# The first stage of a hybrid trunk kernel: adaLN modulation as column sums for three feature tiles and row sums for five, with two head pairs projected tile by tile

## The chip, the cores and the metric

The kernel runs on one core of one Trainium2 chip. The metric is the device time of one execution in microseconds, the median of several runs. The core has five engines that run side by side, each through its own instructions in order: TensorE (PE, matmuls), ScalarE (ACT), VectorE (DVE), GpSimd (POOL) and SyncE (SP), which here issues all transfers between memory and the on-chip buffers. Engines wait for each other through semaphores.

## The reference

One layer of a transformer trunk (DEPTH = 1, so the mixer is stick-breaking attention): 2048 tokens, 1024 features, 16 heads of 64, all float32.

```python
mod_all = jnp.einsum('bd,lde->lbe', jax.nn.silu(c), ada_w) + ada_b[:, None]
sh_m, sc_m, gt_m, sh_f, sc_f, gt_f = jnp.split(mod_all[i][:, None, :], 6, axis=-1)
h = modulate(rms_norm(x, norm_g[i, 0]), sh_m, sc_m)     # h * (1 + scale) + shift
qkv = h @ w_qkv
...
z = q @ k^T * scale ; a = exp(z - reverse_cumsum(softplus(z)))  (masked) ; o = a @ v
...
x = x + gt_m * rms_norm(o @ w_o, norm_g[i, 1])
h = modulate(rms_norm(x, norm_g[i, 2]), sh_f, sc_f)
x = x + gt_f * rms_norm((silu(h @ w_g) * (h @ w_u)) @ w_out, norm_g[i, 3])
```

The change concerns the first three lines and the first two head pairs of the fourth.

## The kernel before

Sequence blocks are 512 tokens wide (`BT`, four blocks `b`), features come in eight tiles of 128 (`KC`, index `k` or `m`), heads in eight pairs `p`. A float32 product is done as three matmuls of rounded high halves and residual low halves (`mm3`, L174): high by high, high by low, low by high. So each operand is split: ACT rounds the high half, DVE subtracts it to get the low half. PE, ACT, DVE and POOL run in the order in which the program text calls them (`manual_schedule`); SP's order is left to the framework. Tiles come from pools by tag with a fixed number of buffers (`BUFS`); taking a buffer whose last user is not done means a wait. SP has eight semaphores for its transfers in turn, so it issues a transfer once the one eight places earlier has landed.

A step `(p, b)` projects one pair's K (`t=1`), Q (`t=0`) and V (`t=2`) for one block, in that order: 3 × 8 × 3 = 72 matmuls, `project` (L453). The steps run (0,0), (1,0), (0,1), (0,2), (0,3) and so on. Step (1,0) is "parked": block 0's normalised input is at hand, so pair 1 is projected with it and its K, Q and V go to memory until pair 1's turn. After each product, `split` (L505) takes one of two buffers with the tag `qkn`, ACT and DVE write its halves, and SP copies them into K's or Q's own layout (four transfers each, L524 and L538) or to memory (parked).

The first stage is what comes ahead of the attention:

- Modulation: shift and scale are `silu(c) @ ada_w` for 2 × 1024 columns, 8 MB of weights. Before, they come in four quarters `q` of two feature tiles (`ada_chunk`, L701). For each quarter DVE sums `c[k]` times row chunk `k` over the chunks into a 128 × 512 sum (`ada_sum`, L719: L724 and L727), PE multiplies the last chunk directly (`ada_direct`, L734: L737) and sums the DVE sums over the partitions (`ada_rest`, L742: L744). Each such matmul has 128 × 128 weights and a single moving column. `ada_cols_done` (L749) adds the biases and makes the gains.
- Block 0: tokens are loaded (`x_load`), their mean squares taken on ACT (`x_square`), scaled on DVE (`x_scale`), transposed on PE (`x_turn`, L367), given gain and shift on ACT (`full_high`, L776), and split (`low`, L789). `first_products` (L768) adds tile `m` to pair 0's three accumulators. The loop over `q` interleaves the sums for the next quarter with the products of this one.
- Step (1,0) then runs as an ordinary step from the stored halves. Its weights come through `split_early` (L207). Around its matmuls lie block 0's stores, block 1's squares and normalisation, and block 2's squares (`SQUARE_AT`).
- Blocks 1 and 3 are normalised from a transposed copy of `x` (`cols_load`, tag `kt`): `x_share` (L355) turns the per-token factors into a row spread over all partitions with four transposes, `scale_cols` (L377) multiplies (even tiles on DVE, odd ones on POOL), and `modulate` (L389) adds the shift and splits. `first_norm` (L420) strings these together, one tile at a time.

Of the kernel before, what the change touches and what calls it, by code (L numbers as in the profile page):

```python
# [9 lines left out]
F32 = mybir.dt.float32  # L10
# [29 lines left out]
SLICES = [0, 3 * KC] + [3 * KC + VGAP] * (NPAIR * NB - 2)  # L40


AHEAD = 6 * KC + 6
# [4 lines left out]

AQ = 256
# [25 lines left out]
SQUARE_AT = [(0, 2), (0, 7), (2, 1), (2, 7)]  # L75

NORM_AT = {
    None: [], 1: [(0, 4), (0, 6), (2, 3), (2, 5)],
    2: [(2, 2), (2, 4), (2, 6)], 3: [(2, 2), (2, 4), (2, 6)],
}  # L80
# [27 lines left out]
def hybrid_trunk_kernel(  # L108
# [5 lines left out]
    ada_first: bass.AP,  # L114
# [28 lines left out]
    shift = const.tile([P, 2, KC], F32, name="shift")  # L143
    c_act = const.tile([P, KC], F32, name="c_act")
# [61 lines left out]

    def split_early(p, t, tags):  # L207

        raw = raws.pop((p, t))
        if len(tags) == 1:  # L210
            hl = att.tile([P, 2, KC, P], F32R, name=f"w{p}_{t}", tag=tags[0], bufs=BUFS[tags[0]])
            hi, lo = hl[:, 0], hl[:, 1]
        else:
            hi, lo = [
                att.tile([P, KC, P], F32R, name=f"w{p}_{t}_{j}", tag=tag, bufs=BUFS[tag])
                for j, tag in enumerate(tags)
            ]
        nc.scalar.copy(hi, raw)
        nc.vector.tensor_tensor(lo, raw, f32(hi), op=ALU.subtract)
        weights[p, t] = hi, lo  # L220

# [86 lines left out]

    def x_load(b):
        for i in range(4):  # L310
            r0 = b * BT + i * P
            if b == 2:
                if i % 2 == 0:
                    pair = att.tile([P, 2, D], F32, name=f"x{b}_{i}", tag="qt", bufs=BUFS["qt"])
                tok = pair[:, i % 2]
# [5 lines left out]
    def cols_load(b):  # L321
        for m in range(KC // 2):
# [54 lines left out]
    def scale_cols(b, k):  # L377
# [4 lines left out]
        if k % 2 == 0:  # L382
# [6 lines left out]
    def modulate(hl, b, k):  # L389

        gain, add = g_eff[:, 0, k : k + 1], shift[:, 0, k : k + 1]
# [7 lines left out]
        if k % 2 == 0:  # L399
# [53 lines left out]
    def project(at):  # L453

        p, b = STEPS[at]
        begun = (p, b) == (0, 0)
# [7 lines left out]
        def product(t):  # L464
            if begun:
                return first_acc[t]
            w = weights[p, t]
            if parked and t == 1:
                acc = zps.tile([P, BT], F32, name=f"pj{p}_{b}_{t}", tag="z")
            else:  # L470
                acc = accps.tile([P, BT], F32, name=f"pj{p}_{b}_{t}", tag="acc")
            ahead = b == NB - 1 and p + 1 < NPAIR
            for k in range(KC):
                if t == 1:
# [4 lines left out]
                    if k == 5 and waiting:  # L479
                        waiting.pop()()  # L480
                if parked and t == 1 and k % 2 == 0:
                    nc.sync.dma_start(*stores[k // 2])
                if parked and (t, k) == (1, 6):
                    split_early(1, 2, ["whl"])
                if nb in (1, 3) and t == 1 and k < 4:
                    x_square(nb, k)
                if nb and t == 1 and 2 <= k < 6:
                    x_spread(nb, k - 2)
                if nb == 2 and (t, k) == (0, 0):
                    x_load(3)  # L490
                if nb == 1 and (t, k) in SQUARE_AT:
                    x_square(2, SQUARE_AT.index((t, k)))
                if nb and (t, k) == (0, 1):
                    x_share(nb)
                if (t, k) in NORM_AT[nb]:
                    first_norm(nb, NORM_AT[nb].index((t, k)))
# [37 lines left out]
        else:  # L534
# [6 lines left out]
            queries[p, b] = qt  # L541

# [154 lines left out]
    chunks, piece_sums, cols_ps = {}, {}, {}  # L697

    ON_PE = {0: (0, KC - 1), 1: (KC - 1,), 2: (KC - 1,), 3: (KC - 1,)}

    def ada_chunk(q, kh):  # L701
        ks = range(KC // 2 * kh, KC // 2 * (kh + 1))
        if q == 2:
            for k in ks:
                w = att.tile([P, 2, AQ], F32, name=f"ac{q}_{k}", tag="a", bufs=BUFS["a"])
                nc.sync.dma_start(w, ada_first[q, kh][:, :, k % 4])
                chunks[q, k] = w
            return
        tag = "ht" if (q, kh) == (1, 1) else "qt"
        w = att.tile([P, 2, KC // 2, AQ], F32, name=f"ac{q}_{kh}", tag=tag, bufs=BUFS[tag])  # L710
        nc.sync.dma_start(w, ada_first[q, kh])
        for k in ks:
            chunks[q, k] = w[:, :, k % 4]

    def ada_begin(q):
        cols_ps[q] = zps.tile([P, BT], F32, name=f"acol{q}", tag="z")
        nc.vector.memset(cols_ps[q][:, :4], 0.0)

    def ada_sum(q, k):  # L719
        w, scale = chunks[q, k], c_act[:, k : k + 1]  # L720
        if q not in piece_sums:
            acc = att.tile([P, 2, AQ], F32, name=f"asum{q}", tag="w", bufs=BUFS["w"])
            piece_sums[q] = acc
            nc.vector.tensor_scalar(acc, w, scale, None, op0=ALU.mult)  # L724
        else:
            acc = piece_sums[q]
            nc.vector.scalar_tensor_tensor(acc, w, scale, acc, op0=ALU.mult, op1=ALU.add)  # L727

    def ada_sums(q):
        return [k for k in range(KC) if k not in ON_PE[q]]  # L730

    COLUMNS = [(2 * seg + j, seg, slice(j * P, (j + 1) * P)) for seg in range(2) for j in range(2)]

    def ada_direct(q, k):  # L734

        for n, seg, js in COLUMNS:
            nc.tensor.matmul(  # L737
                cols_ps[q][:, n : n + 1], chunks[q, k][:, seg, js], c_act[:, k : k + 1],
                start=False, stop=False, skip_group_check=True,
            )  # L740

    def ada_rest(q):  # L742
        for n, seg, js in COLUMNS:
            nc.tensor.matmul(  # L744
                cols_ps[q][:, n : n + 1], piece_sums[q][:, seg, js], ones[:, 0:1],
                start=False, stop=n == 3, skip_group_check=True,
            )

    def ada_cols_done(q):  # L749

        ps, ms = cols_ps.pop(q), slice(2 * q, 2 * q + 2)
        nc.vector.tensor_tensor(shift[:, 0, ms], ps[:, 0:2], b_cols[:, 0, ms], op=ALU.add)
        sc = att.tile([P, KC], F32, name=f"sc0_{q}", tag="sc", bufs=1)[:, :2]
        nc.vector.tensor_tensor(sc, ps[:, 2:4], b_cols[:, 1, ms], op=ALU.add)
        nc.vector.scalar_tensor_tensor(
            g_eff[:, 0, ms], sc, 1.0, gc[:, 0, ms], op0=ALU.add, op1=ALU.mult
        )

    def weights_high(t):
        hl = att.tile([P, 2, KC, P], F32R, name=f"w0_{t}", tag="whl", bufs=BUFS["whl"])  # L760
        nc.scalar.copy(hl[:, 0], raws[0, t])
        weights[0, t] = hl[:, 0], hl[:, 1]

    def weights_low(t):
        hi, lo = weights[0, t]
        nc.vector.tensor_tensor(lo, raws.pop((0, t)), f32(hi), op=ALU.subtract)
# [918 lines left out]
```

## Time and profile before

| | |
|---|---|
| median of 3 runs | 2847.76 us (2846.84 to 2848.67) |
| the profiled execution | 2848.15 us, of which its span is 2845.8 us |
| PE busy (matmul) | 2795.2 us, 98% of the span |
| DVE, ACT, POOL busy | 71%, 57%, 45% |
| HBM traffic | 165 GB/s over the span |
| first 20 us: PE, DVE, ACT busy | 8.33, 9.79, 10.55 us |
| DMA in the first 100 us | 366 GB/s |

How to read it: a timeline row gives the start in us, the time it took, the engine, the line, the operation, output <- inputs, the shape, how many were merged (`x8`), and in brackets how long the engine had been idle and what released it. Consecutive matmuls overlap in these rows, so their pace is the distance between starts. An f32 matmul shows as two rows. `PEld` is the loading of weights, `SPq` SP's issue of a transfer. In the views by stretch, after the length come PE's busy time with the number of rows in parentheses, the granted clock of PE as a share of the full one, the busy share of the DMA engines and GB/s.

### The profile page before, as it was taken

The page shows a single profiled execution, that of the slowest core. Times are in us where ns is not written, and L with a number is a line of the kernel's source. Part 1 is how long each engine was busy: PE and PEld are TensorE (multiplying, and loading weights), DVE is VectorE, ACT ScalarE, POOL GpSimd, SP SyncE. Part 2 cuts the span into 40 slices and gives each one's busy share as a digit, 9 for nine tenths or more (in the row PEclk, how much of TensorE's full clock was granted, in tenths as well). Part 3 has the DMA queues.
Part 4 walks back from the last instruction along what each step waited for, and adds up shares of the span by engine and source line. Part 5 has one row for each costly group of instructions (what it writes and reads, how often), then busy time and mean ns, then how long its engine had stood idle before and what let it go on. Part 6 is the DMA issues. An engine that isn't in the chain of part 4 may idle for free.

```text
span 2845.8 us, 41691 instructions
## 1 busy us (share of the span) xinstructions
PE 2795.2 (98%) x13792; PEld 2330.7 (82%) x13792; DVE 2028.9 (71%) x2821; ACT 1634.1 (57%) x3273; POOL 1289.3 (45%) x2036
## 2 busy tenths in 40 slices
PE   8899999999999999999999999999999999999998
PEld 6688888888888888887888788888788888888887
DVE  6788888888888888888866766555775665133477
ACT  5787777787787877878645533333433333322343
POOL 2575666676576655666410122222222222544455
PEclk9999999999999999999999999999999999999999
DMA  9874556656665635546289544334353334545565
GB/s 368 283 225 164 185 161 221 211 178 226 193 211 186 216 114 178 193 134 230 95 296 317 195 141 151 119 106 158 124 177 108 111 108 163 191 142 155 179 224 185
DMA packets 240519, 521.03 MB, mean 183 GB/s; under 512 B 22448, under 2 KB 110512, under 8 KB 222640
## 3 DMA queue, kind: packets, MB, share of 16 engines
q1 hardware_dynamic: 240304, 518.38, 56.2%
q8 instruction: 109, 1.79, 0.3%
q14 instruction: 106, 0.87, 0.1%
HBM read 351.04 MB, written 118.49 MB: 165 GB/s over the span
## 4 chain that ended last, share of the span: by engine, by line
PE 86%; DVE 5%; ACT 3%; issue 2%; POOL 2%; DMA 2%; SPq 0%; DVEq 0%; POOLq 0%; ACTq 0%
PE s L176 9%; PE s L178 9%; PE s L177 9%; PE z L604 8%; PE o L683 8%; PE t L655 8%; PE pj L176 5%; PE pj L177 5%; PE pj L178 5%; PE o L177 4%; PE o L176 4%; PE o L178 4%; PE y L178 2%; PE y L176 2%; PE y L177 2%
## 5 line engine op out<-in xcount | busy, mean ns | idle before, releaser
L645 POOL TENSOR_TENSOR a<-a,w 128x512 f32<-128x512 f32 (+3 forms) x640 | 621.1, 970 | 225.2 <-DVE w L638 128.9
L638 DVE TENSOR_TENSOR_SCAN w<-z,c,begin 128x512 f32<-128x512 f32 x384 | 489.3, 1278 | 84.6 <-ACT z L623 62.2
L176 PE MATMUL s<-r,l 128*128 128x512 f32 x1232 | 482.2, 391 | 4.8 <-DVE p L1447 3.9
L178 PE MATMUL s<-r,l 128*128 128x512 f32 x1232 | 479.9, 390 | 0.0
L177 PE MATMUL s<-r,l 128*128 128x512 f32 x1232 | 479.9, 390 | 0.0
L621 ACT ACTIVATE a<-z 128x512 f32<-128x512 f32 (+3 forms) x640 | 347.4, 543 | 170.4 <-PE z L604 137.7
L683 PE MATMUL o<-aT,v 128*128 128x512 f32 (+3 forms) x1280 | 384.3, 381 | 0.1
L671 DVE TENSOR_TENSOR aT<-t,aT 128x512 fp32r<-128x512 f32 (+3 forms) x640 | 358.6, 594 | 23.7 <-ACT aT L665 23.0
L604 PE MATMUL z<-kt,qt 128*128 128x512 f32 (+3 forms) x1280 | 363.0, 365 | 0.1
L665 ACT CAST aT<-t 128x512 fp32r<-128x512 f32 (+3 forms) x640 | 314.1, 534 | 73.4 <-PE t L655 63.2
L623 ACT ACTIVATE z<-z 128x512 f32<-128x512 f32 (+3 forms) x640 | 345.0, 539 | 0.0
L1455 POOL TENSOR_TENSOR one<-p,p 128x512 f32<-128x512 f32 x44 | 71.6, 1627 | 578.1 <-issue 321.7
L176 PE MATMUL pj<-ht,w 128*128 128x512 f32 x768 | 309.1, 402 | 5.0 <-issue 1.4
L655 PE MATMUL t<-begin,a 128*128 128x128 f32 x2176 | 295.2, 273 | 14.3 <-DVE aT L671 13.0
L655 PEld LDWEIGHTS t<-begin,a 128*128 128x128 f32 x2176 | 254.7, 140 | 65.1 <-DVE aT L671 15.5
L177 PE MATMUL pj<-ht,w 128*128 128x512 f32 x768 | 303.4, 395 | 1.8 <-DVE ht L408 0.5
L178 PE MATMUL pj<-ht,w 128*128 128x512 f32 x768 | 302.8, 394 | 0.0
L176 PEld LDWEIGHTS s<-r,l 128*128 128x128 f32 x1232 | 231.7, 188 | 54.8 <-ACT l L1308 2.9
L178 PEld LDWEIGHTS s<-r,l 128*128 128x128 f32 x1232 | 231.6, 188 | 48.4
L177 PEld LDWEIGHTS s<-r,l 128*128 128x128 f32 x1232 | 231.8, 188 | 48.2 <-issue 0.5
L633 DVE TENSOR_TENSOR_SCAN w<-z,begin 128x128 f32<-128x128 f32 (+3 forms) x256 | 208.6, 817 | 76.9 <-ACT z L623 66.0
L604 PEld LDWEIGHTS z<-kt,qt 128*128 128x128 f32 x1280 | 230.3, 188 | 37.8 <-DVE w L633 0.5
(178 smaller groups left out, 4866.6 us busy)
## 6 DMA issues: line engine op xcount, KB each, us to landing
ht<-h_s SPq DMA_DIRECT2D x108, 1024.0 KB, 8.4
wi<-in_win SPq DMA_DIRECT2D x86, 512.0 KB, 4.0
qt<-qn SPq DMA_DIRECT2D x124, 256.0 KB, 4.6
ol_qt<-act_s SPq DMA_DIRECT2D x56, 512.0 KB, 3.7
act_s<-S SPq DMA_DIRECT2D x66, 256.0 KB, 3.9
br<-in_wout SPq DMA_DIRECT2D x66, 256.0 KB, 3.5
h_s<-ht SPq DMA_DIRECT2D x16, 1024.0 KB, 8.3
o_s<-os SPq DMA_DIRECT2D x128, 128.0 KB, 2.8
```

Source lines behind the costliest of these rows:

```text
L176: nc.tensor.matmul(acc, lhs[0], rhs[0], start=first, stop=False, **kw)
L177: nc.tensor.matmul(acc, lhs[0], rhs[1], start=False, stop=False, **kw)
L178: nc.tensor.matmul(acc, lhs[1], rhs[0], start=False, stop=last, **kw)
L604: nc.tensor.matmul(z[:, :n], q[:, e, part, r * P : (r + 1) * P], k[:, e, :n], start=part == 0, stop=part == 1,)
L621: nc.scalar.activation(a[:, :n], z[:, :n], AF.Sigmoid, scale=QK_SCALE)
L623: nc.scalar.activation(z[:, :n], z[:, :n], AF.Sigmoid, scale=-QK_SCALE)
L638: nc.vector.tensor_tensor_scan(rest[:, rev], left[:, rev], begin[:, :BT][:, rev], initial=carries[r], op0=ALU.mult, op1=ALU.bypass,)
L645: nc.gpsimd.tensor_tensor(a[:, :n], a[:, :n], rest[:, 1 : n + 1], op=ALU.mult)
L655: nc.tensor.transpose(pt[:, rb * P : (rb + 1) * P], weighed[i, rb][:, j * P : (j + 1) * P], ident)
L665: nc.scalar.copy(hl[:, 0, t0:], pt[:, t0:])
L671: nc.vector.tensor_tensor(hl[:, 1, t0:], pt[:, t0:], f32(hl[:, 0, t0:]), op=ALU.subtract)
L683: nc.tensor.matmul(acc[:, t0:], lhs, hl[:, part, t0:], start=sc == qb and j == 0 and part == 0, stop=sc == 0 and j == 3 and part == 1,)
```

## The change

Modulation by feature tile `m`, not by quarter. Tiles 0 to 2 (`COLUMNS = 3`) are summed on PE alone: for shift and scale each eight matmuls with a single moving column, into one PSUM tile `acol`. Tiles 3 to 7 come with `ada_w` transposed, features on partitions, and DVE multiplies a 128 × 1024 tile by `silu(c)` spread over all partitions and accumulates along the row in one instruction (`row_sum`); the spread `c_rows` is made by two PE matmuls of ones and `c_line` (`c_spread`) and copied by ACT. `row_load` makes two loads of 512 KB for a tile, shift and scale. `row_done` makes `mod` and `g_eff` of one tile.

```diff
-    def ada_chunk(q, kh):
...
-    def ada_cols_done(q):
...
+    ROW_TAGS = {0: "whl", 1: "qt", 2: "qt", 3: "qt", 4: "ht", 5: "ht"}
+    def row_load(m):
...
+    def column(m, seg):
+        w = rows[m][seg].rearrange("p (k f) -> p k f", f=P)
+        out_col = acol[:, 2 * m + seg : 2 * m + seg + 1]
+        for k in range(KC):
+            nc.tensor.matmul(out_col, w[:, k], c_act[:, k : k + 1], start=k == 0, stop=k == KC - 1)
+    def row_sum(m, seg):
+        nc.vector.scalar_tensor_tensor(
+            w, w, 1.0, c_rows, op0=ALU.mult, op1=ALU.mult, accum_out=sums[m][:, seg : seg + 1])
+    def row_done(m):
+        total = acol[:, 2 * m : 2 * m + 2] if m < COLUMNS else sums.pop(m)
+        nc.vector.tensor_tensor(mod[:, :, m], total, b_cols[:, 0:2, m], op=ALU.add)
+        nc.vector.scalar_tensor_tensor(g_eff[:, 0, m : m + 1], mod[:, 1, m : m + 1], 1.0, ...)
```

Both pairs' products of block 0 are then made tile by tile, with six accumulators (pair 1's in the three buffers of `zps`): `products(p, m, *ts)` in place of `first_products(m)`, and steps (0,0) and (1,0) no longer yield (`begun = at < 2`, `SLICES = [0, 0, ...]`). The loop over `q` gives way to a list of calls. Its core:

```diff
+    column(0, 0); column(0, 1)
...
+    column(1, 0); column(1, 1)
+    turn_x(0); turn_x(1); row_done(1)
+    weights_high(0, 1); full(0); weights_low(0, 1); weights_high(0, 0); high(0); full(1)
+    turn_x(2); weights_low(0, 0)
+    column(2, 0)
+    low(0); weights_high(0, 2); turn_x(3); weights_low(0, 2)
+    products(0, 0, 1, 0)
+    high(1); weights_high(1, 1); low(1)
+    column(2, 1)
+    products(0, 0, 2); products(0, 1, 1)
+    weights_low(1, 1); row_done(2); weights_high(1, 0)
+    products(1, 0, 1); products(0, 1, 0)
...
+    products(0, 2)
+    row_sum(4, 0); row_sum(4, 1); row_done(4); low(3); full(4); high(4)
+    products(1, 2)
...
+    products(0, 6)
+    x_share(1)
+    products(1, 6)
+    products(0, 7)
+    first_norm(1, 0); first_norm(1, 1)
+    products(1, 7)
```

In `project`, pair 0's K and Q splits are each preceded by one more `first_norm` of block 1, the loads of block 2 and two stores of block 0 follow pair 0's Q, and `split` for pair 1 (parked) comes right behind. The two V turns run at `k` = 3 and 5 of step (0,1)'s K product. Block 2's squares move from step (1,0) to the Q product of step (0,1).

```diff
         def product(t):
             if begun:
-                return first_acc[t]
+                if at == 0 and t != 2:
+                    first_norm(1, 2 + (t == 0))
+                return first_acc[p, t]
...
-                    if k == 5 and waiting:
-                        waiting.pop()()
+                    if k in (3, 5) and waiting:
+                        waiting.pop(0)()
...
-                if nb in (1, 3) and t == 1 and k < 4:
+                square_at = {2: 0, 3: 1}.get(nb)
+                if t == square_at and k < 4:
                     x_square(nb, k)
...
+        if at == 0:
+            x_load(2)
+            store(2)
+            store(3)
```

For block 1, `scale_cols` and `modulate` treat all tiles as the even ones were (`if k % 2 == 0 or b == 1`): DVE scales, ACT adds the shift and rounds, DVE makes the low half. Buffers change hands: the raw weights of pair 1 take the tag `v`, those of pair 0's V the tag `kt`, `c_line` and `c_rows` the tag `qkn`. SP's order in the changed kernel is: tile 0's rows, `c`, block 0's tokens, biases, tile 1's rows, pair 0's weights, tile 2's rows, pair 1's weights, the rows of tiles 3 to 7, then block 1's transposed copy and tokens and block 0's stores. The attention and everything behind it are unchanged.

More of the change, by code (lines that the diff above doesn't have):

```diff
@@ L47 @@
 EAGER = 12
-AQ = 256
 BUFS = {
@@ L764, in weights_low @@
[L764 to L770 removed]
+                out_col, w[:, k], c_act[:, k : k + 1], start=k == 0, stop=k == KC - 1,
+            )
+    def row_sum(m, seg):
+        w = rows[m][seg]
+        if m not in sums:
+            sums[m] = att.tile([P, 2], F32, name=f"as{m}", tag="as", bufs=3)
+        nc.vector.scalar_tensor_tensor(
+            w, w, 1.0, c_rows, op0=ALU.mult, op1=ALU.mult, accum_out=sums[m][:, seg : seg + 1]
+        )
@@ L824, in hybrid_trunk_kernel @@
+    column(0, 1)
+    c_spread = [zps.tile([P, BT], F32, name=f"cs{half}", tag="z") for half in range(2)]
+    for half in range(2):
+        nc.tensor.matmul(
+            c_spread[half], ones, c_line[:, half * BT : (half + 1) * BT], start=True, stop=True
+        )
+    c_rows = att.tile([P, D], F32, name="c_rows", tag="qkn", bufs=BUFS["qkn"])
+    x_square(0, 0)
+    row_done(0)
+    for i in range(1, 4):
         x_square(0, i)
         x_scale(0, i - 1)
+    for half in range(2):
+        nc.scalar.copy(c_rows[:, half * BT : (half + 1) * BT], c_spread[half])
@@ new lines, in hybrid_trunk_kernel @@
+    row_done(6)
+    low(5)
+    products(0, 4)
+    products(1, 4)
+    turn_x(7)
+    cols_load(1, 2)
+    cols_load(1, 3)
+    store(0)
+    store(1)
+    full(6)
+    high(6)
+    row_sum(7, 0)
+    row_sum(7, 1)
+    row_done(7)
+    low(6)
+    x_square(1, 0)
+    products(0, 5)
+    products(1, 5)
+    full(7)
+    high(7)
+    low(7)
+    for i in range(1, 4):
+        x_square(1, i)
+        x_spread(1, i - 1)
+    x_spread(1, 3)
+    products(0, 6)
+    x_share(1)
+    products(1, 6)
```

348 lines of the change are left out of this document (166 added, 182 removed).

## The prediction

> **What bounds the kernel now.** I read the page first, then TensorE (PE) in order of time over the first 100 us, then its busy time and granted clock in stretches, then the groups by line.
>
> ```profile
> span 2845.8 us, 41691 instructions
> PE   8899999999999999999999999999999999999998
> PE 86%; DVE 5%; ACT 3%; issue 2%; POOL 2%; DMA 2%; SPq 0%; DVEq 0%; POOLq 0%; ACTq 0%
> ```
>
> PE carries 86% of the chain that ended last. So whatever moves the point at which PE gets through a given product early on moves the end by about as much. I measure the change at one such point: the end of the first product (K, `t=1`) of step (0,1), the third step. Behind it the work on PE is the same in both kernels.
>
> ```profile
> 20.56 0.80 PE L176 MATMUL pj<-ht,w 128*128 128x512 f32 x1 [0.67 <-ACT ht L786]
> ...
> 69.98 0.39 PE L178 MATMUL pj<-ht,w 128*128 128x512 f32 x1
> 70.21 0.39 PE L176 MATMUL pj<-ht,w 128*128 128x512 f32 x1
> ...
> 76.52 0.59 ACT L507 CAST kn<-pj 128x512 fp32r<-128x512 f32 x1 [1.32 <-PE pj L178]
> ```
>
> Products begin at 20.56. Steps (0,0) and (1,0), 72 matmuls each, are through at 70.2, and the K product of (0,1) at about 76.35 (ScalarE, ACT, was waiting for it until 76.52). The clock matters in between:
>
> ```profile
> 6.23 1.84 PE L737 MATMUL acol<-c_act,ac 128*128 128x1 f32 x8 [6.23 <-DMA ac<-in_ada_first]
> ...
> 23.74 0.63 PE L176 MATMUL pj<-ht,w 128*128 128x512 f32 x1
> 24.16 0.63 PE L177 MATMUL pj<-ht,w 128*128 128x512 f32 x1
> ...
> 42.16 0.60 PE L372 MATMUL xT<-begin,xn 128*128 128x128 f32 x4
> 42.60 0.95 PE L737 MATMUL acol<-c_act,ac 128*128 128x1 f32 x8
> ```
>
> A product matmul starts every 0.43 us early on and every 0.23 us later (69.98 to 70.21); eight one-column rows (four f32 matmuls, two rows each) take 1.84 us early and 0.95 us later. Both are a factor of two, a half clock. The stretches (length, PE busy, granted clock, DMA share, GB/s) show when:
>
> ```profile
> 9.30:12.72 3.42, 2.86 (x14) 1.00 1.03 422
> ...
> 26.37:29.79 3.42, 3.02 (x22) 1.00 1.11 403
> 29.79:33.20 3.41, 3.41 (x9) 0.50 0.98 405
> ```
>
> From 29.79 to 33.20 the clock is written as 0.50 and nine matmuls fill 3.41 us. Ahead of that it is written as 1.00 although the spacing is the slow one, so there I go by the spacing. Two readings follow. In 9.30 to 12.72 PE was busy for 84% with columns, and they stayed slow. In 26.37 to 29.79 it was busy for 88%, a good part of it columns, and lost the full clock. Columns do not seem to keep the clock up; streamed 512-wide matmuls do.
>
> **The change part by part.** *Ahead of the products.* Before, the path held 24 column rows ahead of the transposes. Now PE's order is columns (0,0), (0,1), two spreads of `c`, columns (1,0), (1,1), transposes of tiles 0, 1 and 2, column (2,0), transposes of tile 3, and only then the first product. A column is eight f32 matmuls, 16 rows: 3.7 us slow (2 × 1.84), 1.9 full.
>
> ```profile
> 25.02 1.05 PE L372 MATMUL xT<-begin,xn 128*128 128x128 f32 x4
> 25.87 1.20 PE L737 MATMUL acol<-c_act,ac 128*128 128x1 f32 x8
> ...
> 433.42 1.13 PE L293 MATMUL ap<-aacc,ones 128*128 128x512 f32 x2 [0.70 <-DVE v L557]
> 433.98 1.03 PE L683 MATMUL o<-aT,v 128*128 128x512 f32 x2
> ```
>
> Four transposes take 0.85 slow and 0.44 full, start to start; an f32 512-wide spread is two rows in 0.56 full, near the product's pace, so four rows slow are about 1.7. Data are no limit there:
>
> ```profile
> 9.89 1.06 ACT L167 ACTIVATE xn<-x 128x1024 f32<-128x1024 f32 x1 [5.68 <-DMA x<-in_x]
> 16.45 1.04 ACT L761 CAST w<-wr 128x1024 fp32r<-128x1024 f32 x1 [0.34 <-DMA wr<-in_wqkv]
> 19.08 0.78 ACT L782 ACTIVATE hf<-xT,shift,g_eff 128x512 f32<-128x512 f32 x1 [1.59 <-PE xT L372]
> ```
>
> The fifth load of 512 KB landed at 9.9 and the tenth at 16.45: 1.31 us each. By that pace the first now lands at about 4.9, the eighth (second half of tile 1's modulation) at 13.8, the twelfth (tile 2's first half) at 19.1. With the slow clock: 4.9 + 2 × 3.7 = 12.3, + 1.7 = 14.0, + 2 × 3.7 = 21.4, tile 0's transposes 22.25, seen by ACT at 22.45; the first `full` (0.78) 23.2, which frees a bank for tile 2's transposes to 24.05, column (2,0) to 27.75, tile 3's to 28.6. ACT and VectorE (DVE) split the weights meanwhile. **The first product starts at 28.6, 8.0 us later than now.** Bounds for the unknown, the clock under unbroken columns: full from about 8.4 on gives 21.2 (the twelfth load, 19.1, + 1.9 + 0.4 sets it), never full 28.6. I take 28.6, by the 84% stretch.
>
> *Both pairs tile by tile.* From there PE has no reason to wait long: 144 × 0.23 = 33.1, column (2,1) 1.9, transposes of tiles 4 to 7 1.8, the row spread 0.4: 37.2 at full clock. The first six matmuls are slow (+1.2), and column (2,1) right behind them is again a stretch without streaming, which in the 26.37 stretch cost a slow window: 3.41 us at half, +1.6. Sum 40.0, so PE is through both steps at **E = 68.6** against 70.2. Bounds +1.2 and +5.6 (column slow, two slow windows): 67.0 to 71.4.
>
> That holds if DVE delivers. Ten `row_sum` instructions over 1024 columns with an accumulated output are new, and no row shows one.
>
> ```profile
> L727 DVE SCALAR_TENSOR_TENSOR asum<-ac,c_act,asum 128x512 f32<-128x512 f32 x23 | 17.3, 750 | 1.0 <-DMA ac<-in_ada_first 0.4
> L766 DVE TENSOR_TENSOR w<-wr,w 128x1024 fp32r<-128x1024 f32 x3 | 3.6, 1221 | 0.1
> L755 DVE SCALAR_TENSOR_TENSOR g_eff<-sc,gc 128x2 f32<-128x2 f32 x4 | 0.6, 160 | 0.1
> L791 DVE TENSOR_TENSOR ht<-hf,ht 128x512 fp32r<-128x512 f32 x8 | 5.5, 689 | 2.5 <-ACT ht L786 2.2
> ```
>
> 512 more columns cost 1.22 - 0.69 = 0.53, so it takes 0.75 + 0.53 = 1.28; lower bound 1.22, upper bound at two cycles per column 0.75 + 3 × 0.53 = 2.34. I take 1.3, nearest to a row of the same operation. Per tile DVE then needs two of these, two small ones (0.16 each) and a low half (0.69), 3.6 us, and PE 18 × 0.23 + 0.44 = 4.6: hidden. The Trainium skill, Vector Engine (DVE) Microarchitecture Reference, "Points that are easy to get wrong", says that a scalar-tensor-tensor with two non-bf16 SBUF sources runs at half throughput. The 23 rows with such sources took 0.75 us, not the 1.28 that halving gives, so without an accumulated output the trace speaks against it; with one it is open.
>
> *Parking.* Before, pair 1's K and Q were split after (1,0) had run, long after pair 0's. Now both pairs end together. The split tiles have two buffers, so pair 1's K split waits until pair 0's four K copies have landed, and its Q split until the Q copies have. On ACT and on DVE those two stand ahead of tiles 4 to 7 of block 1, which PE needs from the fifth matmul group of (0,1) on.
>
> ```profile
> 58.16 0.60 PE L363 MATMUL xr<-begin,x 128*128 128x128 f32 x4
> 58.79 0.59 ACT L365 COPY x<-xr 128x512 f32<-128x512 f32 x1 [0.37 <-PE xr L363]
> ```
>
> The Q copies of before (a view of the tile `qt`; SP's issues, then from issue to landing), and rows of ACT and DVE around them:
>
> ```profile
> L538 SPq DMA_DIRECT2D qt<-qn x4: 540/619/1316, 54.0 to 55.9; - x4
> DMA to landing us min/median/max: 3.0/4.5/5.5
> 65.55 0.57 ACT L507 CAST qn<-pj 128x512 fp32r<-128x512 f32 x1
> 67.26 0.74 DVE L383 SCALAR_TENSOR_TENSOR xc<-xc,g_eff,x 128x512 f32<-128x512 f32 x1
> 67.92 0.74 DVE L401 SCALAR_TENSOR_TENSOR ht<-xc,shift,ht 128x512 fp32r<-128x512 f32 x1
> 81.99 0.59 ACT L507 CAST qn<-pj 128x512 fp32r<-128x512 f32 x1 [4.88 <-PE pj L178]
> ```
>
> Block 1's row spread starts 18 + 9 matmuls and its own four ahead of E: E - 6.6. The copy ends 1.2 us later, then twelve DVE instructions at 0.66 (67.26 to 67.92) (six scalings, four low halves, pair 0's K and Q) end at E + 2.6. SP then issues the four Q copies; the last goes 1.9 us after the first and lands up to 5.5 later: **E + 10**. Bounds: 3.0 for a quiet queue, E + 8; with the 1 MB store of block 1 that now stands just ahead, E + 12. Now the same wait is covered: 65.55 is some 4 us behind the last landing. Then ACT splits Q, copies V, makes tile 4 (some 0.6 each, by 65.55 and 58.79), DVE the low half: PE resumes at E + 11.8 after idling since E + 3. Four groups of three, with one set of transposes among them, take 3.2 full and 6 slow after such a pause; with the low halves arriving every 0.66 and the clock back on the way I take 5.3: K is done at **E + 17.1 = 85.7** against 76.35: **+9.4 us**.
>
> *The rest* hides: block 2's squares moved to (0,1)'s Q product stand where ACT now waits 4.9 us for PE (81.99), the stores and `x_load(2)` follow on SP behind the Q copies and are needed 10 us later. All scalings of block 1 on DVE cost nothing further; they are among the twelve.
>
> Sum: 2848.15 (the profiled run, span 2845.8 and 2.35 around it) + 9.4 = 2857.5. That run is 0.4 above the median 2847.76, so I predict **2857.1**.
>
> **The rivals.**
>
> *The clock comes up under the columns.* For it: PE is busy without a gap from 4.9 on, while the 84% stretch had gaps. Against: the 88% stretch that lost the clock. The first product is then at 21.2, E at 58.4 (37.2 behind it), K done at 75.5 with the same parking: -0.9, 2846.9. The Trainium skill, TensorE: Matmul & The Clock Gate, Part 1, says that PE starts at half clock and gets the full one after a window of about 3.4 us of sustained activity. By that rule alone the columns would suffice; the 9.30 stretch is the row against it.
>
> *Parking doesn't hold PE* (the Q copies land before DVE gets there, or later slack gives the idle time back). Against: the order of instructions on ACT and DVE, and a landing at E + 8 at the earliest while PE has work only to E + 3. With E = 68.6, and K 6.15 later as now, it is done at 74.75: -1.6, 2846.2.
>
> *Both of these*: E 58.4, K at 64.55: -11.8, 2836.0, the gain that the two pairs' interleaving holds.
>
> *`row_sum` at 2.34.* DVE needs 5.7 per tile against PE's 4.6; over five tiles PE waits about 6 us: +15.4, 2863.2. It decides from 1.8 us on, where the tile costs 4.6.
>
> **How the numbers follow.** Forecast (K from 67.0 + 15.1 to 71.4 + 19.1, +6 to +14, 2853.5 to 2861.9): 0.62. Row sums slow: 0.07. Early clock alone: 0.13. No parking wait alone: 0.08. Both: 0.10. About 0.2% (5.7 us) can be told from no change. Slower takes the forecast's upper 0.61 and the 0.07: 0.68; faster the 0.10 and 0.01 of the two cases before it: 0.11; within: 0.21. The range 2845 to 2862 leaves out the double gain and half of the slow row sums.
>
> **What would show it.** In the changed profile: `column` rows of eight at 1.84 us up to 21 us (right) or 0.95 (clock rival); first product near 28.6; a PE gap of 8 to 9 us in the K product of (0,1), ended by tile 4's ACT or DVE work, with DVE's `qn` behind a Q copy; `row_sum` at 1.3. A first product before 23 or a gap under 4 us would make the prediction wrong.

## The result and the profile after

| | median | lowest to highest | runs |
|---|---|---|---|
| before | 2848.63 us | 2846.84 to 2853.41 | 12 |
| changed | 2857.20 us | 2852.76 to 2862.15 | 12 |

The ratio is 1.0030, 95% interval 1.0022 to 1.0038: 0.3% slower, 8.6 us. The changed kernel's profiled execution took 2858.29 us (before: 2848.15), so it lies in the upper half of its runs. Its page, the lines that answer to the first three of before:

```profile
span 2856.3 us, 41748 instructions
PE   8899999999999999999999999999999999999998
PE 84%; DVE 6%; issue 3%; DMA 2%; ACT 2%; POOL 2%; SPq 1%; DVEq 0%; POOLq 0%; ACTq 0%
```

Over the whole span little looks different: PE's share of the chain is 2% smaller, ACT's 1% smaller, and those of DVE, SP and "issue" are 1% larger each. The place is found in PE's timeline of the first 90 us:

```profile
5.16 6.95 PE L706 MATMUL acol<-c_act,ar 128*128 128x1 f32 x32 [5.16 <-DMA ar<-in_ada_cols_first]
11.98 3.76 PE L804 MATMUL cs<-c_line,ones 128*128 128x512 f32 x4
15.53 6.83 PE L706 MATMUL acol<-c_act,ar 128*128 128x1 f32 x32
...
25.09 3.41 PE L706 MATMUL acol<-c_act,ar 128*128 128x1 f32 x16
...
29.11 0.78 PE L174 MATMUL pj<-ht,w 128*128 128x512 f32 x1
...
31.60 1.84 PE L706 MATMUL acol<-c_act,ar 128*128 128x1 f32 x16
...
66.90 0.39 PE L176 MATMUL pj<-ht,w 128*128 128x512 f32 x1
67.13 0.39 PE L174 MATMUL pj<-ht,w 128*128 128x512 f32 x1
...
73.12 1.11 PE L539 MATMUL vt<-begin,vT 128*128 128x128 f32 x4 [3.77 <-DVE kn L491]
...
80.69 0.79 PE L174 MATMUL pj<-ht,w 128*128 128x512 f32 x1 [5.17 <-ACT ht L389]
```

Up to 29.11 PE works almost without a break, on columns at the slow pace (32 rows in 6.95 us, 0.217 each; 16 rows in 1.84 at full clock). The products of both pairs then run to 67.1 in 38.0 us; before, they took from 20.56 to 70.2, 49.6 us. Behind that stand two gaps. The first ends with DVE's `kn`: pair 0's V turn needs a PSUM buffer of the pool `zps`, which pair 1's K accumulator holds until it is split. The second ends with ACT's work on tile 4. ACT's own rows say what holds the splits:

```profile
71.76 0.58 ACT L490 CAST kn<-pj 128x512 fp32r<-128x512 f32 x1 [4.86 <-DMA kt<-kn]
78.94 0.58 ACT L490 CAST qn<-pj 128x512 fp32r<-128x512 f32 x1 [6.60 <-DMA qt<-qn]
...
87.27 0.59 ACT L490 CAST kn<-pj 128x512 fp32r<-128x512 f32 x1 [2.94 <-DMA k_park<-kn]
```

The first two are pair 1's K and Q splits, each behind a copy of pair 0's; the third is the K split of step (0,1), 10.75 us later than before (76.52); its product had ended some 0.3 us earlier, at about 86.9. The row sums, DVE in groups by line:

```profile
L714 DVE SCALAR_TENSOR_TENSOR ar<-ar,c_rows 128x1024 f32<-128x1024 f32 x10 | 11.9, 1220 | 0.0
...
L714 DVE DVE_READ_ACCUMULATOR ar<-ar,c_rows 128x1 f32 x10 | 0.8, 82 | 0.0
```

From here on four points of the timeline are compared: the first product; the start of block 1's row spread (`xr`, 6.6 us ahead of the end of both steps in the changed order); ACT's K split of (0,1); block 3's row spread, in step (0,2). The four points are given in us, from each kernel's profiled execution; the ratio is that to runs of the kernel before on the same chip.

| kernel | first product | spread 1 | K split | spread 3 | profiled | median | ratio, 95% interval |
|---|---|---|---|---|---|---|---|
| before | 20.56 | (other order) | 76.52 | 103.57 | 2848.15 | 2848.63 |  |
| changed | 29.11 | 60.52 | 87.27 | 114.35 | 2858.29 | 2857.20 | 1.0030 (1.0022 to 1.0038) |
| own_buffers | 25.94 | 57.60 | 72.88 | 108.19 | 2852.90 | 2856.83 | 1.0029 (1.0018 to 1.0039) |
| one_column | 19.65 | 55.25 | 81.63 | 108.72 | 2854.73 | 2854.35 | 1.0020 (1.0011 to 1.0028) |
| warm_up | 29.70 | 61.08 | 87.52 | 114.60 | 2856.91 | 2858.82 | 1.0039 (1.0026 to 1.0052) |
| own_buffers_one_column | 19.57 | 55.18 | 70.45 | 105.79 | 2851.24 | 2851.40 | 1.0008 (0.9999 to 1.0016) |
| early_x2 | 26.14 | 61.51 | 88.98 | 116.06 | 2859.02 | 2859.42 | 1.0040 (1.0027 to 1.0053) |
| own_buffers_early_x2 | 24.25 | 54.63 | 69.91 | 101.57 | 2844.33 | 2852.50 | 1.0019 (1.0009 to 1.0028) |
| own_early_one_column | 19.70 | 55.33 | 70.61 | 100.09 | 2845.80 | 2846.27 | 0.9992 (0.9982 to 1.0001) |
| three_edits_gpsimd | 19.82 | 59.02 | 74.30 | 106.01 | 2850.99 | 2851.37 | 1.0006 (0.9997 to 1.0016) |
| x3_early | 19.65 | 55.26 | 70.53 | 108.61 | 2857.17 | 2854.68 | 1.0017 (1.0008 to 1.0026) |
| x3_and_spread_early | 19.47 | moved | 68.84 | 108.07 | 2850.12 | 2854.87 | 1.0017 (1.0008 to 1.0026) |
| three_edits_spread_early | 19.80 | moved | 68.67 | 101.77 | 2848.74 | 2844.94 | 0.9983 (0.9974 to 0.9992) |
| x3_early_cols_held | 19.78 | 55.41 | 70.70 | 103.37 | 2853.39 | 2854.16 | 1.0018 (1.0009 to 1.0027) |

The column "profiled" is the time of the execution that the four points come from. It can be far from the median: own_buffers_early_x2's is the fastest of its ten runs, three_edits_spread_early's the slowest of its eleven. From block 3's row spread to the end these executions took between 2742.1 and 2750.0 us, so the four points alone don't settle a difference of a few microseconds in the time.

### The profile page after: what moved, and what is told of

The parts are those of the page before. It is cut to its first block, busy times and chain, and to the rows that moved or that the text cites. A ratio compares the mean times of both kernels' runs of the same rounds, so it can differ in the third digit from the quotient of the medians.

```text
span 2856.3 us, 41748 instructions
## 1 busy us (share of the span) xinstructions
PE 2806.4 (98%) x13820; PEld 2343.9 (82%) x13820; DVE 2022.1 (71%) x2819; ACT 1632.8 (57%) x3272; POOL 1280.1 (45%) x2032
## 4 chain that ended last, share of the span: by engine, by line
PE 84%; DVE 6%; issue 3%; DMA 2%; ACT 2%; POOL 2%; SPq 1%; DVEq 0%; POOLq 0%; ACTq 0%
PE s L174 9%; PE s L175 9%; PE s L176 9%; PE z L591 8%; PE o L670 8%; PE t L642 8%; PE pj L174 6%; PE pj L176 6%; PE pj L175 6%; PE o L176 4%; PE o L175 4%; PE o L174 4%; PE y L176 1%; PE y L174 1%; PE y L175 1%
## 5 line engine op out<-in xcount | busy, mean ns | idle before, releaser
L642 PEld LDWEIGHTS t<-begin,a 128*128 128x128 f32 x2176 | 255.1, 141 | 63.4 <-DVE aT L658 14.3
```

What stands on the lines that cost most here:

```text
L642: nc.tensor.transpose(pt[:, rb * P : (rb + 1) * P], weighed[i, rb][:, j * P : (j + 1) * P], ident)
```

## The experiments

The theory to be tested: the 8.6 us are a start that is 8.5 us later (columns on PE at half clock), 11.6 us won back by the interleaving, and some 11 to 13 us of waiting behind both steps, because the parked splits share two buffers with pair 0's.

**own_buffers.** The parked splits take two buffers of a tag that is free by then.

```diff
-            hl = att.tile([P, 2, BT], F32R, name=f"{tag}n{p}_{b}", tag="qkn", bufs=BUFS["qkn"])
+            place = "aT" if parked else "qkn"
+            hl = att.tile([P, 2, BT], F32R, name=f"{tag}n{p}_{b}", tag=place, bufs=BUFS[place])
```

> The changed kernel with the K and Q splits of the parked step in two buffers of the tag aT (free once pair 1's products are through) instead of the two that pair 0's splits use; nothing else. Theory (the wait for pair 0's copies is what parking costs): the 5.0 to 7 us that ScalarE's kn and qn splits of pair 1 wait for the copies kt<-kn and qt<-qn are gone, and with them the 3.8 us gap ahead of pair 0's V-turn and most of the 5.2 us gap ahead of tile 4. PE is through both steps at 67.1 as in the changed kernel, and the K product of (0,1) is done at 73.3 to 75.5 instead of 86.95 (6.15 behind that point in the kernel before, up to 2 more if VectorE is late with tile 4). Time 2857.2 - 11.5 to - 13.6: 2843.6 to 2845.7, some 3 to 5 us below the kernel before. Rival 1 (ScalarE and VectorE are late with block 1's tiles 4 to 7 anyway, because scalings, splits and low halves of both pairs fall together): a gap of 4 to 5 us ahead of tile 4 stays, K done at 79 to 82, time 2849 to 2852. Rival 2 (later slack gives the idle time back): K done early, time 2856 to 2858 all the same.

The waits went as expected: spread 1 to K split is 15.3 us instead of 26.75, and the V turn waits for nothing. The time did not follow: 2856.8, the value of rival 2. PE's timeline and ACT's of this kernel show where the 11.5 us went:

```profile
84.02 0.47 PE L361 MATMUL xT<-begin,x 128*128 128x128 f32 x1 [4.22 <-DVE x L338]
85.19 0.47 PE L361 MATMUL xT<-begin,x 128*128 128x128 f32 x1 [0.69 <-DVE x L338]
```

```profile
72.88 0.59 ACT L491 CAST kn<-pj 128x512 fp32r<-128x512 f32 x1 [1.21 <-issue]
78.15 1.06 ACT L165 ACTIVATE xj<-x 128x1024 f32<-128x1024 f32 x1 [4.68 <-DMA x<-in_x]
...
81.95 1.06 ACT L165 ACTIVATE xj<-x 128x1024 f32<-128x1024 f32 x1 [1.40 <-DMA x<-in_x]
```

ACT now stands for block 2's tokens. SP issued them behind pair 0's Q copies:

```profile
67.40 5.11 SPq L522 DMA_DIRECT2D qt<-qn  x4
72.55 2.88 SPq L307 DMA_DIRECT2D x<-in_x  x4
```

K split to spread 3 was 27.05 us before, 27.08 in the changed kernel, and is 35.31 here: 8.2 of the 11.5 us are given back. It isn't rival 2's slack, for ACT's rows show a second wait, which the first had covered; own_buffers_early_x2, below, tests it.

**one_column.** Tile 0 alone as columns; tiles 1 and 2 as row sums.

```diff
-COLUMNS = 3
+COLUMNS = 1
...
-    column(1, 0)
-    column(1, 1)
...
+    low(0)
+    row_sum(1, 0)
+    row_sum(1, 1)
+    row_done(1)
...
-    column(2, 0)
...
-    column(2, 1)
...
     weights_low(1, 1)
+    row_sum(2, 0)
+    row_sum(2, 1)
     row_done(2)
```

> The changed kernel with the modulation of tile 0 alone as column sums on PE, of tiles 1 to 7 as row sums on VectorE (tile 1's behind the low half of tile 0, tile 2's behind the split of pair 1's K weights), both buffers of the parked step as they are. Theory (the start is late because the columns run on PE at the slow clock ahead of the products): without 32 + 16 column matmuls ahead of them (6.8 and 3.4 us) the first product starts at 20.5 to 21.5 instead of 29.1, VectorE becomes what sets the first two tiles, PE is through both steps at 59.5 to 61.5 instead of 67.1, and the parking wait stays about 19.8 behind that: time 2857.2 - 5.5 to - 7.5: 2849.7 to 2851.7. Rival 1 (loads of weights and modulation set the start, not PE): first product at 25 or later, both steps through at 64 to 67, time 2854 to 2857. Rival 2 (VectorE with 14 row sums can't keep up): PE idles for over 6 us between the first product and the end of both steps, time 2856 to 2860.

First product at 19.65, spread 1 at 55.25 (both steps through at 61.9, 5.3 earlier), K split to spread 3 unchanged (27.09). So the start is set by the columns, not by loads. But the median fell by 2.9 only, to 2854.35 where 2849.7 to 2851.7 were expected. The profiled execution has spread 3 5.6 us earlier than the changed kernel's and is 3.6 us shorter, so some 2 us are lost behind that point. The 29.11 of the changed kernel is also one execution only; that others start sooner, as three kernels with the same start do (below), would account for a part of the rest, but isn't shown.

**warm_up.** Six 512-wide f32 matmuls on zeros ahead of the first column.

```diff
+    warm = tps.tile([P, BT], F32, name="warm", tag="t")
+    for _ in range(6):
+        nc.tensor.matmul(warm, ones, begin[:, :BT], start=True, stop=True)
     column(0, 0)
```

> The changed kernel with six 128x512 f32 matmuls on zeros ahead of the first column, into a bank that nobody reads: added work of 5.2 us at the slow pace, from some 2 us on. Theory (streamed 512-wide matmuls bring the clock up, one-column matmuls don't keep it): the columns of tile 0, which then start at 7 to 7.5, run at the full pace for one window, 32 rows in 3.7 us instead of 6.95 until the clock falls, and tile 1's columns are slow again (6.8 us): first product at 26.5 to 29.5, time 2854.5 to 2857.5. Rival 1 (any unbroken busy time brings it up, and the changed kernel's start was only too short or broken): columns of tile 0 and of tile 1 at the full pace, first product at 22 to 24, time 2850 to 2852. Rival 2 (the clock comes up at a set time after the start, about 26 to 31 us, whatever PE does): all columns at 6.8 to 7 us, first product at 31, time 2859.

PE's timeline, then the stretches (length, PE busy, and after the other engines the granted clock, DMA share, GB/s):

```profile
1.94 8.41 PE L802 MATMUL warm<-begin,ones 128*128 128x512 f32 x12 [1.94 <-POOL begin masks.py:199]
10.19 3.63 PE L706 MATMUL acol<-c_act,ar 128*128 128x1 f32 x32
13.68 2.65 PE L807 MATMUL cs<-c_line,ones 128*128 128x512 f32 x4
16.12 6.83 PE L706 MATMUL acol<-c_act,ar 128*128 128x1 f32 x32
```

```profile
11.40:14.80 3.40, 3.40 (x25) 2.92 (x25) 0.91 (x4) 2.05 (x4) 0.45 (x1) 1.00 1.03 416
14.80:18.20 3.40, 3.40 (x13) 2.43 (x12) 2.52 (x6) 2.12 (x3) 2.46 (x3) 0.50 1.02 410
18.20:31.80 13.60, 13.58 (x60) 12.80 (x60) 6.25 (x8) 7.21 (x9) 0.00 (x0) 0.50 1.03 408
```

Tile 0's columns ran at full pace behind streamed matmuls (3.63 instead of 6.95); with PE busy throughout, the clock fell at 14.8 and stayed at half until 31.8. That is the theory's order of events and against rivals 1 and 2. The matmuls took 8.4 us instead of the 5.2 expected. They held the first column back by 5.0 us (10.19 instead of 5.16) and brought 4.4 from there to the first product: 29.7, just outside 26.5 to 29.5, and at 2858.8 the time is 1.3 above the range expected.

The clock may also explain part of the spread of the changed kernel's runs. Up to the first product, PE's order is the same in the changed kernel, own_buffers, early_x2 and own_buffers_early_x2; it came at 29.11, 25.94, 26.14 and 24.25. In own_buffers the two spreads of `c` brought the clock up and tile 1's columns ran at full pace:

```profile
11.93 3.51 PE L805 MATMUL cs<-c_line,ones 128*128 128x512 f32 x4
15.27 3.91 PE L707 MATMUL acol<-c_act,ar 128*128 128x1 f32 x32
```

The Trainium skill, TensorE: Matmul & The Clock Gate, Part 1, says that the activity window is 3.4 us long and free-running. This case agrees: in own_buffers the recorded clock is 0.50 from 18.46 to 28.70, three times 3.41 us. Counted back from 18.46 in such steps, one window lasts from 11.64 to 15.05 and holds 3.1 us of spreads. In the changed kernel the recorded changes at 72.3 and 85.9 and the change of the products' pace at 31.3 lie on one such grid (twelve and four steps apart); counted back on it, a boundary falls at 14.3, and the spreads lie 2.3 and 1.3 us on either side of it. That fits with 3.5 us of spreads being enough in one execution and not in the other. The run-to-run spread as a whole was not traced. Runs of the kernel before spread over 5.1 to 8.1 us too, those with one column over 4.6 to 7.4, those with three columns, where there were at least ten, over 9.4 to 13.8; what else makes these spreads stays open.

**own_buffers_one_column.** Both edits.

> Both edits at once: the parked step's K and Q splits in buffers of the tag aT, and only tile 0's modulation as columns. If the two costs are separate (the start on PE, the parking behind both steps), the savings add: PE through both steps at 59.5 to 61.5, the K product of (0,1) done 6.5 to 8.5 behind that, time 2857.2 - 17 to - 21: 2836 to 2840, some 9 to 12 us below the kernel before. Rival (one limit behind both: block 1's loads or VectorE's scalings of block 1 set the K product of (0,1), whichever way PE gets there): the saving is that of the larger edit alone, 2843 to 2847.

Up to the K split the two do add: it comes 14.4 us earlier with own_buffers (2.9 of them from its earlier start), 5.6 with one_column and 16.8 with both, and from spread 1 it is 15.3 us as with own_buffers. In the time 5.8 us are left (2.9 and 0.4 alone), far from 17 to 21, since 8.3 us behind the K split are given back again (35.34 to spread 3).

**early_x2 and own_buffers_early_x2.** Block 2's load ahead of pair 0's copies, with the shared buffers and with buffers of their own.

```diff
     x_load(1)
+    x_load(2)
     row_sum(6, 1)
...
         if at == 0:
-            x_load(2)
             store(2)
```

> The changed kernel with the load of block 2's tokens issued right behind block 1's (some 46 us in) instead of behind pair 0's Q copies (75 us); the parked step's buffers as in the changed kernel. Theory (two waits side by side: PE is held by the parked splits first, and block 2's late load is hidden behind that wait): nothing is gained while the parked splits hold ScalarE and VectorE. K product of (0,1) still some 19.8 us behind the end of both steps, block 2's transposes right behind the queue of work as before, time 2855 to 2858.5. Rival (the late load alone costs the 7 to 10 us): time 2847 to 2850. Rival (the copies of K and Q land sooner without the load behind them, or later with the stores): time 2852 to 2862.

> Parked splits in buffers of their own, and block 2's load issued early; columns as in the changed kernel. With buffers alone the K product of (0,1) was done 9.1 us behind the end of both steps instead of 19.8, but block 2's transposes then stood idle for 4.2 + 0.7 + 0.2 + 0.4 us for tokens that landed from 78 us on, and the next six matmuls ran at half clock. Theory (that load is what was hidden): those gaps go, block 3's row spread comes 36 to 38 us behind the end of both steps (33.4 in the kernel before, 47.2 in the changed one, 44.0 with buffers alone), time 6 to 8 us below buffers alone: 2849 to 2851 as a median, with a spread of some 10 us. Rival (block 2's squares on ScalarE or its scalings on VectorE are late by themselves): gaps ahead of block 2's transposes stay above 3 us, time 2854 to 2857.

With shared buffers it brings nothing (27.08 from K split to spread 3, and 27.5 ahead of it; 2859.4, just above the range). With own buffers spread 3 comes 31.7 behind the K split instead of 35.3, so 3.7 of the 8.2 us are won back, and the gaps ahead of block 2's transposes are gone. Behind the end of both steps it comes at 40.3, not at 36 to 38, and the median of 2852.5 is above the 2849 to 2851 expected. By the medians removing one wait alone brings 0.4 us or nothing and both 4.7, each uncertain by some 3 us or more. The profiled executions, counted from behind the start, show the same more clearly: from spread 1 to spread 3 it is 53.8 us in the changed kernel, 50.6 with own buffers, 54.6 with the early load and 46.9 with both. So the two waits do lie side by side. The next one had appeared, 3.40 us ahead of tile 6 of block 2: ACT now stands for block 3's tokens.

**own_early_one_column and three_edits_gpsimd.** The three edits; then three low parts of weights on GpSimd, to unburden DVE.

```diff
-        nc.vector.tensor_tensor(lo, raws.pop((p, t)), f32(hi), op=ALU.subtract)
+        eng = nc.gpsimd if (p, t) in ((0, 2), (1, 1), (1, 0)) else nc.vector
+        eng.tensor_tensor(lo, raws.pop((p, t)), f32(hi), op=ALU.subtract)
```

> All three edits: parked splits in buffers of their own, block 2's load early, tile 0 alone as columns. The end of both steps at 61.8 as with one column, block 3's row spread 36 to 38 us behind that at 98 to 100 (103.6 in the kernel before): 3.5 to 5.5 us below the kernel before, 2843 to 2845.5. Rival (block 2's load now competes with the stores and block 1's loads, and block 1's squares are late): the end of both steps moves to 64 or later, time 2847 to 2850.

> The three edits, and the low parts of three weights (pair 0's V, pair 1's K and Q) on GpSimd, 2.4 us each by the rows of later weights, instead of VectorE (1.22 each), with tile 2's row sums moved up into the room. With one column VectorE was busy without a break from 20 to 43 us and PE waited for it until tile 2 at 39.8. Theory (VectorE sets the first two tiles there): tile 2's products begin at 33 to 36, the end of both steps at 56 to 59, time 3 to 5.5 us below the three edits: 2838 to 2842. Rival (GpSimd and VectorE slow each other, 128x1024 rows of VectorE at 1.5 us or more): no gain, 2843 to 2848.

The three edits gave 2846.3, 0.8 above the expected range, no longer slower than before but not surely faster (0.9992, to 1.0001). GpSimd made it 5 us worse, 2851.4, above even the rival's 2843 to 2848; both steps are through at 65.6, not at 56 to 59. GpSimd's rows, then DVE's:

```profile
20.79 2.55 POOL L741 TENSOR_TENSOR w<-wr,w 128x1024 fp32r<-128x1024 f32 x1 [4.47 <-ACT w L736]
24.01 2.62 POOL L741 TENSOR_TENSOR w<-wr,w 128x1024 fp32r<-128x1024 f32 x1 [0.67 <-ACT w L736]
30.65 3.06 POOL L741 TENSOR_TENSOR w<-wr,w 128x1024 fp32r<-128x1024 f32 x1 [4.03 <-ACT w L736]
```

```profile
21.02 3.40 DVE L714 SCALAR_TENSOR_TENSOR ar<-ar,c_rows 128x1024 f32<-128x1024 f32 x1
...
24.35 3.35 DVE L714 SCALAR_TENSOR_TENSOR ar<-ar,c_rows 128x1024 f32<-128x1024 f32 x1
...
28.02 1.22 DVE L714 SCALAR_TENSOR_TENSOR ar<-ar,c_rows 128x1024 f32<-128x1024 f32 x1
...
31.53 2.21 DVE L720 TENSOR_TENSOR mod<-as,b_cols 128x2 f32<-128x2 f32 x1
```

The two row sums that meet a GpSimd subtraction end 1.1 us behind it (24.42 behind 23.34, 27.70 behind 26.63): they ran when it was through. An addition of two elements per partition took 2.21 us and ended with the third subtraction, at 33.7.

**x3_early, x3_and_spread_early, three_edits_spread_early, x3_early_cols_held.** Two further moves: block 3's tokens ahead of the K copies of (0,1), and block 1's squares and row spread one product group earlier; then the second alone, and the first with block 3's columns held back behind the Q copies of (0,2).

```diff
-                if nb == 2 and (t, k) == (0, 0):
+                if nb == 2 and (t, k) == (1, 4):
                     x_load(3)
```

```diff
     products(0, 5)
+    for i in range(1, 4):
+        x_square(1, i)
+        x_spread(1, i - 1)
     products(1, 5)
     full(7)
     high(7)
+    x_spread(1, 3)
     low(7)
-    for i in range(1, 4):
-        x_square(1, i)
-        x_spread(1, i - 1)
-    x_spread(1, 3)
-    products(0, 6)
     x_share(1)
+    products(0, 6)
```

> The three edits (parked splits in buffers of their own, block 2's load early, tile 0 alone as columns; VectorE makes all low parts), and block 3's token load ahead of the K copies of (0,1) on SP instead of behind them (some 75 us instead of 83). With the three edits ScalarE stood 1.5 us for block 3's tokens (until 87.9) with tile 6's modulation of block 2 queued behind it, and PE 1.6 us behind that. Theory (each earlier end makes the next load the late one): that gap goes, time 1 to 2 us below the three edits' 2846.3: 2844.3 to 2845.3, 2.5 to 3.5 below the kernel before. Rival (the K copies of (0,1), now behind 2 MB of loads, land later and the first scores wait): no gain or a loss of 1 to 2, 2846 to 2848.

> As the run before, and three squares and the row spread of block 1 one product group earlier (squares ahead of tile 7's modulation on ScalarE, the spread ahead of pair 0's tile 6 products on PE). VectorE's chain of scalings, low halves and four splits starts at block 1's row spread and ended 1.5 us late for tile 5 of (0,1). Theory (that chain sets the end of the K product of (0,1), 9.1 us behind both steps instead of 6.15): it starts some 2 us earlier, the 1.5 us gap goes, time 1.5 to 2 below the run before: 2842.5 to 2843.5. Rival (tile 7's modulation, now behind the squares, is late for its products, or block 1's tokens are not there yet): a new gap of 1 to 3 us ahead of the row spread or tile 7, time 2844 to 2848.

> The three edits (own buffers, block 2's load early, one column) with block 3's load where it was, and the three squares and the row spread of block 1 one product group earlier, as in the run with both moves. Theory (VectorE's chain behind the row spread sets the end of the K product of (0,1)): the 1.5 us gap goes, as it did there, and the time is 1 to 2 us below the three edits' 2846.3: 2844.3 to 2845.3. Rival (the earlier K product only makes block 3's tokens later by comparison): ScalarE's wait for them grows from 1.5 to 3 us and the time stays at 2845.8 to 2847.

> As the run with block 3's token load ahead of the K copies, but block 3's 2 MB of transposed columns are loaded behind the Q copies of (0,2) instead of ahead of that step's products. There PE stood 10.6 us for the Q copies of (0,2), which took 11.8 us from issue to landing against 5.9 with the three edits, with the columns issued at 85 to 90 us ahead of them. Theory (bulk loads queued ahead of the small copies are what made them late): the copies land 5 to 7 us after their issue, the 10.6 us wait is under 1 us, time back to 2844.3 to 2846, 8 to 10 us below that run. Rival 1 (the next weights' loads at 92 to 94 us ahead of them are enough): copies still 9 us or more, time 2850 to 2853. Rival 2 (the columns are now late for block 3's first tiles): a gap of 2 to 4 us ahead of (0,3), time 2847 to 2849.

The first move is a miss of over 9 us (2854.7), and with the second move on top of it one of over 11 (2854.9). Block 3's gap went, and PE stood for something else. Its timeline in x3_early, then SP's issues and the copies of `qt` from 85 us on, first there, then in own_early_one_column:

```profile
108.16 0.66 PE L591 MATMUL z<-kt,qt 128*128 128x128 f32 x2 [10.59 <-DMA qt<-qn]
```

```profile
85.41 5.12 SPq L313 DMA_DIRECT2D xc<-in_xt  x4
...
94.63 4.18 SPq L522 DMA_DIRECT2D qt<-qn  x4
...
L522 SPq DMA_DIRECT2D qt<-qn x4: 462/464/467, 94.6 to 98.3; - x4
...
DMA to landing us min/median/max: 10.8/11.8/12.7
```

```profile
93.23 3.21 SPq L522 DMA_DIRECT2D qt<-qn  x4
96.48 3.21 SPq L313 DMA_DIRECT2D xc<-in_xt  x4
...
L522 SPq DMA_DIRECT2D qt<-qn x7: 461/596/1225, 93.2 to 111.3; - x7
...
DMA to landing us min/median/max: 5.4/5.9/6.9
```

The tokens' early issue let SP run ahead, so that block 3's columns (`xc`) and the next weights were queued in front of the small Q copies. Holding the columns back brought the wait down to 5.15 us with copies that still took 10.4 (rival 1), and moved 6.92 us of waiting for the columns to DVE (rival 2): no gain, 2854.2. The second move alone has the lowest median, 2844.94: faster than before by 0.17% (0.9983, 0.9974 to 0.9992) and about 12 us below the changed kernel. Against the three edits (0.9992) the intervals overlap. The 1.5 us gap is gone as expected, and the K split comes 1.9 us earlier. But ACT's wait for block 3's tokens grew to 2.40, and PE now waits for the Q copies of (0,2) as well:

```profile
101.31 0.66 PE L591 MATMUL z<-kt,qt 128*128 128x128 f32 x2 [2.75 <-DMA qt<-qn]
```

By spread 3 the profiled execution has lost the 1.9 us again (101.77 against 100.09), so it is not shown that this gain reaches the end.

## Why the prediction was right

The time was 2857.1 predicted, 2857.2 measured, and the mechanism, a later start, a faster interleaving and a wait for shared buffers, is the one that the rows show. The agreement to 0.1 us is luck: the runs spread over 9.4 us, and in the profiled execution E came 1.5 us earlier and the rest of the K product 2.7 us later than predicted. Against the kernel before it is 9.3 us predicted and 8.6 measured. One price that the forecast did not need was wrong.

- *Columns ahead of the products*: right. First product at 28.6 predicted, 29.11 measured. The spread of `c` was mis-sized: taken at 1.7 us, it took from 11.98 to 15.53, 3.55. The 0.56 us for two rows at full clock was a misreading: the two rows themselves start 0.53 apart (433.42 and 433.95), and the next operation's row is recorded only 0.03 behind the second. The columns made up 1.7 us: 6.82, 6.69 and 3.27 us from start to start, where 7.4, 7.4 and 3.7 were charged.
- *Both pairs tile by tile*: E = 68.6 predicted, 67.1 measured. The slow window charged for column (2,1), +1.6, was not paid: behind 31.3 the products ran at full pace. The row sum was 1.22 us, 1.14 from start to start, against 1.3, and DVE stayed hidden. The halved throughput that the Trainium skill states for this form (Vector Engine (DVE) Microarchitecture Reference, "Points that are easy to get wrong") does not show here with an accumulated output either.
- *Parking*: the mechanism was right, the size was not: K done at E + 17.1 predicted, some E + 19.8 measured, beyond the E + 19.1 of the forecast's upper end. SP issued the last of the four Q copies 3.8 us behind the first (70.3 to 74.1), not 1.9, and they landed at about 78.9, E + 11.8, near the upper bound of 12. And the 8.8 us idle were not one gap but two, 3.77 and 5.17: the first, pair 0's V turn waiting for the PSUM buffer of pair 1's K, the text did not name. own_buffers shows that both come from the shared buffers.
- *The rest hides*: true as long as parking holds PE, and the text named no price for the case without that cover. There 8.2 us are lost again by block 3's row spread, first to block 2's load behind the Q copies; issuing it early won back 3.7 of them with three columns and 5.9 with one. So the rival "parking doesn't hold PE" was priced wrongly at 2846.2: own_buffers is that case and took 2856.8.
- *The clock rival*: wrong as put (the columns don't bring the clock up), but in three of the four executions with this start the spreads of `c` raised it for one window, worth some 3 to 5 us at the first product.

In sum the start cost 8.55 us, the interleaving brought 11.6, and the K split of (0,1) came 20.1 us behind the end of both steps instead of 6.3. Of these 13.8 us, own_buffers removes 11.5, and x3_and_spread_early and three_edits_spread_early show 2 more to be DVE's chain behind block 1's row spread. With own buffers alone 8.2 us are lost again behind the K split.

## What to carry to other kernels

When a wait is to be removed, look at what has been issued behind its cover: here a 2 MB load behind eight small copies took back 8.2 of the 11.5 us won, and with either wait removed the other kept most of the loss. A queue that gets ahead of its consumers isn't free either: bulk loads issued early stand in front of the small copies that the next matmul needs. And two stages that ended far apart share buffers at no cost only until they are made to end together.

## What the runs showed of the hardware

- GpSimd and DVE, each with two operands in SBUF, took turns: a 1.22 us row sum took 3.40 and 3.35 us beside GpSimd subtractions of some 2.6. The Trainium skill, SBUF — State Buffer, "SBUF: two separate sides", describes the port pair of the two as an exclusive lock; the rows agree.
- One-column matmuls kept PE busy for 6.95 us without a break at an unchanged 0.217 us a row, while 6 us of 512-wide ones brought the full clock, and columns then lost it. Busy time in the profile is not what the clock goes by. Nor does it take 512 columns: in own_buffers_early_x2 the recorded clock is 0.50 from 18.8 to 22.2 only, and PE spent all but some 0.5 us of that on twelve rows of f32 transposes, with 128 moving columns each.
- An f32 matmul with 512 columns takes about 0.89 us per row at the slow pace (four in 3.55), twice a product's 0.43; in warm_up such rows start 0.85 us apart up to 7.2 us and 0.43 apart from 8.04 on.
